# Hybrid decoder layer on one core: three first output tiles in turn instead of two, input and output moved in pairs of tiles

## The chip, the cores and the metric

One core of one Trainium2 chip runs the whole program. The metric is device time in microseconds (us) of one execution. PE is the matrix engine (TensorE), DVE the vector engine, ACT the scalar engine, POOL the GpSimd engine, SP the engine that here only issues transfers (its queue is SPq; ACT and POOL have queues of their own, ACTq and POOLq).

## The reference, cut to what matters

One layer of a decoder with three kinds of heads, on a prompt of 256 tokens and 8 samples of 8 tokens, so on T = 320 token columns, with a model width D = 2048:

```python
hn = rms_norm(x, norm_mix)
proj = hn @ w_in                      # 2048 x 6656
p_rw, p_hg, p_lru = split(proj)       # RWKV-7 | HGRN2 | RG-LRU
x = x + concat([rwkv7_mix(p_rw), hgrn2_mix(p_hg), rglru_mix(p_lru)]) @ w_out
hn = rms_norm(x, norm_ffn)
gte, val = split(hn @ ffn_w_up)       # 2 x 5632
x = x + (silu(causal_dwconv(gte)) * val) @ ffn_w_down
y = rms_norm(x, norm_final)
```

The RWKV part has 12 heads of 64 columns (a shift by one token, a low-rank decay, a normalised key, a recurrence with a delta rule), the HGRN2 part 6 heads of 128, the RG-LRU part 512 channels. All states and the results are outputs too.

## The kernel before, in words

**Tiles and chunks.** Everything is held transposed: 128 rows of a width on the partitions, the 320 tokens along the free axis. x is 16 tiles of 128x320 (k = 0 to 15). A weight matrix comes in chunks of 128x1024 values (512 KB): eight blocks of 128x128, for eight k-tiles of one output tile. `load` (L167) issues a chunk's transfer on SPq into `raw`. `split_weights` turns it into two parts: ACT casts it (`wh`, L173), DVE subtracts (`wl`, L174). The activations are split likewise into `xh` (ACT, L217) and `xl` (DVE, L218).

**A gemm.** `gemm` makes one output tile from two chunks. Per chunk it issues 16 products `wh` x `xh` and `wh` x `xl` (L198, L199) and then 8 products `wl` x `xh` (L205): 48 products of 128x128 by 128x320 for one output tile. There are 9600 of them in the program; the text calls a place in the program by how many of them stand ahead of it (its count). The result sits in a PSUM buffer of the pool `acc`, which has two, or of `aux_r`, which has four.

**Between the gemms.** All other PE work (about 1000 small fp32 products for the recurrences) is written as generators in queues named n r f h l y; `tick` (at every fourth k-tile and at the end of a chunk) lets a generator go on when its due time, kept in units of an estimated clock, has come. That fixes at which count a step's products stand in PE's stream. A scheduler then orders the instructions of each engine; what goes through `keep_in_program_order` (and `behind`, the same for a transfer on SPq) stays where it was written.

**The head.** Three idle products (L260) run on zeros. SPq issues the first chunks and the 16 tiles of x, one transfer each of 160 KB. `first_tiles` (L307, L308, L310) makes output tiles 0 and 1 (the inputs of the decay and the gate) in turn, four k-tiles at a time, so that work starts when a quarter of x is there. Their PSUM is `aux_r`. Then `rwkv_front` makes tile 3, the key of the first pair of RWKV heads, as an ordinary gemm in `acc`. Behind it stands one product of a matrix of ones with `ssq` (L401), the sum of squares of x, which gives the norm factor `rstd` (ACT L234, DVE L235). With `rstd` the function `shifted` empties the PSUM of tiles 0, 1 and 3 in that order (DVE L378, L380), then come the receptance and value tiles (2 and 4) and the tiles of the first HGRN2 head. POOL issues the loads of `shift`, `h0` and `ccv` at the start, and the loads of masks (`mskf`), `lw` and `s` go on SPq behind the norm product.

**A pair of RWKV heads.** `rwkv_pair` is run six times, alternating with the six HGRN2 heads. Its steps: low-rank products (L482), the key's norm, whose product is L502 (the text says the bones product, from the name of its matrix) with DVE L503, ACT L504 and L505 (Ln and Exp, each with a load of a function table) and DVE L510 behind it; then the operands `nb`, `a`, `BK`, `ARs` (DVE L512 to L556); the chunk products (L578), a triangular solve over 16x16 blocks whose off-diagonal blocks are moved through DRAM (`du`, `U`, L614, L615) and come back in front of PE's transposes L686; and doubling steps (L703), in which PE multiplies 64x64 blocks, ACT copies `Z` (L708) and DVE writes the result into `U` and `T` (L695, by a masked copy). The doubling steps of one pair stand beside the key's norm of the next pair.

**The end.** After the mix come the output projection, the two FFN matrices and the final norm (PE L1282, L1283; ACT L234; DVE L235, L1289, L1291); the 16 result tiles are sent by 16 transfers of 160 KB (L1292), odd ones from ACT's queue, even ones from SP's.

Of the kernel before, what the change touches and what calls it, by code (L numbers as in the profile page):

```python
# [17 lines left out]
P = 128  # L18
# [48 lines left out]
def kernel(ctx: ExitStack, tc: tile.TileContext, i: dict, o: dict):  # L67
# [30 lines left out]
    for h in range(2):  # L98
        for n in range(2):
            chunks.append((i["w_in"][n, h], 8))  # L100
    for n in [c for k, m in ORDER for c in
                       {"r": (3 + 3 * m, 2 + 3 * m, 4 + 3 * m), "h": range(20 + 4 * m, 24 + 4 * m),
                        "l": (44 + 4 * m, 46 + 4 * m, 45 + 4 * m, 47 + 4 * m)}[k]]:
        for h in range(2):
            chunks.append((i["w_in"][n, h], 8))
# [82 lines left out]

    def gemm(pieces, xh, xl, k0=0, first=True, last=True, ps=None):
        if ps is None:  # L190
            ps = acc_p.tile([P, 512], F32, tag="acc", name="acc")
        for c, kc in enumerate(pieces):
            prefetch()
            wh, wl = splits.pop(state["used"])
            state["used"] += 1
            for k in range(kc):
                st = first and c == 0 and k == 0
                PE.matmul(ps[:, :T], wh[:, k, :], xh[k0 + k], start=st, stop=False)  # L198
                PE.matmul(ps[:, :T], wh[:, k, :], xl[k0 + k], start=False, stop=False)  # L199
                state["clock"] += 2 * GEMM_COST  # L200
                if k % 4 == 3:
                    tick()
            for k in range(kc):
                en = last and c == len(pieces) - 1 and k == kc - 1
                PE.matmul(ps[:, :T], wl[:, k, :], xh[k0 + k], start=False, stop=en)  # L205
# [58 lines left out]
    xh, xl, xr = [], [], []  # L264
    ssq = et("ext", T)
# [4 lines left out]

    raws[3] = rp.tile([P, 10, P], F32, tag="big", name="raw3", bufs=BB)
    for g in range(4):
        ks = slice(4 * g % 8, 4 * g % 8 + 4)
        if g < 3:
            load(2 * (g // 2), ks)
        for k in range(4 * g, 4 * g + 4):
            t = yp.tile([P, T], F32, tag=f"y{k}", name="xr")
            SY.dma_start(out=t, in_=i["xT"][k])
            xr.append(t)
        if g == 3:  # L280
            load(2, ks)
        load(2 * (g // 2) + 1, ks)
    for g in range(4):
        ks = slice(4 * g % 8, 4 * g % 8 + 4)
        split_weights(2 * (g // 2), ks)
# [5 lines left out]
        split_weights(2 * (g // 2) + 1, ks)  # L291
        if g:
            squares(range(4 * g - 4, 4 * g) if g < 3 else ())
# [4 lines left out]
    state["raw"] = state["split"] = 4  # L298

    def first_tiles():  # L300

        pss = [aux_r(), aux_r()]
        for g in range(4):
            for n, ps in enumerate(pss):
                wh, wl = splits[2 * (g // 2) + n]
                for k in range(4 * g, 4 * g + 4):
                    PE.matmul(ps[:, :T], wh[:, k % 8, :], xh[k], start=(k == 0), stop=False)  # L307
                    PE.matmul(ps[:, :T], wh[:, k % 8, :], xl[k], start=False, stop=False)  # L308
                for k in range(4 * g, 4 * g + 4):
                    PE.matmul(ps[:, :T], wl[:, k % 8, :], xh[k], start=False, stop=(k == NK - 1))  # L310
            state["clock"] += 24 * GEMM_COST
            if g % 2:
                for n in range(2):
# [81 lines left out]
    def rwkv_front():  # L395
        ps_0, ps_1 = first_tiles()
        tc.keep_in_program_order(V.tensor_scalar(omu, prm[:, PRM["mu"]:PRM["mu"] + 20], -1.0, 1.0, op0=ALU.mult, op1=ALU.add))
        squares(range(8, NK))
        ps_k = gemm(W_CHUNKS, xh, xl)
        ps_n = aux_h()  # L400
        tc.keep_in_program_order(PE.matmul(ps_n[:, :T], ones, ssq, start=True, stop=True))  # L401
# [12 lines left out]
        free(xo)  # L414
        x, xo = shifted(1, ps_1)
        S.activation(sg, x, AF.Sigmoid)
        free(xo)
        return ps_k

# [39 lines left out]

    def rwkv_pair(p, ps_k=None):  # L460
        lw = rp.tile([P, 3, P], F32, tag="lw", name="lw", bufs=2)
# [4 lines left out]
        for name, n in (("k", 3), ("r", 2), ("v", 4)):  # L466
            ps = gemm(W_CHUNKS, xh, xl, ps=aux_r()) if p == 0 and name == "v" else ps_k
            ps_k = None
            box[name] = shifted(n + 3 * p, ps)
# [4 lines left out]
    def rwkv_operands(p, lw, box):  # L474
# [6 lines left out]
        for n, ps in enumerate((ps_w, ps_a)):  # L481
            PE.matmul(ps[:, :T], lw[half[n], n, :], lora[half[n], :], start=True, stop=True)  # L482
        sw = ft("sw")
# [337 lines left out]
    def rwkv_norm(p, lw, y, bo):  # L821
# [20 lines left out]
        PE.matmul(ps_g[:, :T], lw[:, 2, :], sg, start=True, stop=True)  # L842
        yo = yp.tile([P, T], F32, tag=f"y{p}", name="yo")
        V.tensor_tensor(yo, ps_g[:, :T], bo, op=ALU.mult)
# [32 lines left out]
    def hgrn_steps(n, box):  # L877
# [147 lines left out]
        V.tensor_tensor(rs, ps_o[:, :T], rs, op=ALU.mult)  # L1025
        yo = yp.tile([P, T], F32, tag=f"y{NPAIR + n}", name="yo")
        V.scalar_tensor_tensor(yo, rs, pc("hnw", n), g, op0=ALU.mult, op1=ALU.mult)
# [76 lines left out]
    def lru_steps(m, box):  # L1104
        tiles = (2 * m, 2 * m + 1)
        rs, ths, aes = [], [], []
        for n, (xc, _) in zip(tiles, box["x"]):
            w = rp.tile([P, 2, P], F32, tag="wg", name="wg", bufs=1)
            G.dma_start(out=w, in_=i["wg"][n])
            yield L_LRU  # L1110
# [34 lines left out]
        for j, (n, hs) in enumerate(zip(tiles, rs)):  # L1145
# [3 lines left out]
            S.activation(gt, gt, AF.Gelu_apprx_tanh)  # L1149
            yo = yp.tile([P, T], F32, tag=f"y{NPAIR + NHG + n}", name="yo")  # L1150
            hp, hs_ = extended(hs)
# [34 lines left out]

    ps_k = rwkv_front()
    spawn("y", y_steps())
    for kind, n in ORDER:
# [4 lines left out]
        if (kind, n) == ("r", 0):  # L1194
            rwkv_pair(0, ps_k)
        else:
            {"r": rwkv_pair, "h": hgrn_head, "l": lru_pair}[kind](n)
# [7 lines left out]
    def x2_tile(n, ps):  # L1205
        t = yp.tile([P, T], F32, tag=f"y{n}", name="x2")
        G.dma_start(out=t, in_=i["xT"][n])
        V.tensor_tensor(t, ps[:, :T], t, op=ALU.add)
# [77 lines left out]
    for n in range(NK):  # L1286
# [10 lines left out]
NIDLE = 3  # L1297
L_FIRST = 11.0
L_FIRST_OPS = 4.0
# [21 lines left out]
ORDER = [(k, n) for n in range(6) for k in "rh"] + [("l", 0), ("l", 1)]  # L1321
NFIRST = 4
QUEUES = "nrfhly"
BX = 1

_OUTS = {
    "yT": (NK, P, T), "p_rwkv": (NPAIR, P, 64), "s_rwkv": (NPAIR, P, SB, 64), "nshift": (P, 20, 9),
    "p_hgrn": (NHG, P, P), "s_hgrn": (NHG, P, SB, P), "nh": (P, NLRU, 9), "nccv": (P, NLRU, 9, 3),
# [140 lines left out]
```

## Time and profile before

| what | value |
| --- | --- |
| median of 3 runs | 1626.79 us (1625.04 to 1627.25) |
| the profiled execution's own time | 1627.56 us |
| its span in the trace | 1625.8 us |
| PE busy | 1601.6 us, 99% of the span |
| DVE busy | 973.9 us, 60% |
| ACT busy | 809.6 us, 50% |
| POOL busy | 144.7 us, 9% |
| DMA, mean | 147 GB/s |

The profile is of one execution; 1.76 us of its time lie around the span. A row of the timeline has the start, the duration, the engine and line, the operation, and in square brackets how long the engine had been idle and what released it. A matrix product's rows overlap, since products are pipelined: the distance from one start to the next is what it costs. An fp32 product is two passes and shows as two (x2). The granted clock of PE is 0.997 over the span.

### The profile page before, as it was taken

The page shows a single profiled execution, that of the slowest core. Times are in us where ns is not written, and L with a number is a line of the kernel's source. Part 1 is how long each engine was busy: PE and PEld are TensorE (multiplying, and loading weights), DVE is VectorE, ACT ScalarE, POOL GpSimd, SP SyncE. Part 2 cuts the span into 40 slices and gives each one's busy share as a digit, 9 for nine tenths or more (in the row PEclk, how much of TensorE's full clock was granted, in tenths as well). Part 3 has the DMA queues.
Part 4 walks back from the last instruction along what each step waited for, and adds up shares of the span by engine and source line. Part 5 has one row for each costly group of instructions (what it writes and reads, how often), then busy time and mean ns, then how long its engine had stood idle before and what let it go on. Part 6 is the DMA issues. An engine that isn't in the chain of part 4 may idle for free.

```text
span 1625.8 us, 29013 instructions
## 1 busy us (share of the span) xinstructions
PE 1601.6 (99%) x11478; PEld 1548.6 (95%) x11478; DVE 973.9 (60%) x1965; ACT 809.6 (50%) x1280; POOL 144.7 (9%) x364
## 2 busy tenths in 40 slices
PE   9999999999999999999999999999999999999996
PEld 8888989898989999999999999999999999999996
DVE  7786878777776765555555554343455555554444
ACT  7766766676766964443434343323334343344442
POOL 2101111111111300001111110000011110000000
PEclk9999999999999999999999999999999999999998
DMA  8444343444344554454445444555444444445553
GB/s 266 154 132 135 117 141 120 128 120 136 114 135 122 168 169 150 151 158 148 151 148 156 145 153 144 147 152 149 155 151 154 146 153 145 155 146 156 149 151 109
DMA packets 87791, 238.91 MB, mean 147 GB/s; under 512 B 16712, under 2 KB 31096, under 8 KB 87656
## 3 DMA queue, kind: packets, MB, share of 16 engines
q1 hardware_dynamic: 81496, 221.01, 44.4%
q0 software_dynamic: 4576, 14.16, 2.6%
q8 instruction: 90, 1.47, 0.4%
q10 hardware_dynamic: 1584, 1.89, 0.3%
q14 instruction: 45, 0.37, 0.1%
HBM read 225.66 MB, written 11.37 MB: 146 GB/s over the span
## 4 chain that ended last, share of the span: by engine, by line
PE 85%; ACT 7%; DVE 4%; DMA 2%; issue 2%; SPq 0%; POOL 0%; DVEq 0%; ACTq 0%
PE acc L198 26%; PE acc L205 26%; PE acc L199 26%; DVE wl L174 1%; PE aux_r L703 1%; PE aux_h L914 1%; ACT wh L173 1%; DMA raw<-in_w_in 1%; ACT L935 0%; ACT L893 0%; ACT L1023 0%; DVE x L1289 0%; PE aux_r L656 0%; PE aux_r L729 0%; DMA mskf<-in_msk 0%
## 5 line engine op out<-in xcount | busy, mean ns | idle before, releaser
L173 ACT CAST wh<-raw 128x1024 fp32r<-128x1024 f32 (+2 forms) x412 | 421.6, 1025 | 542.8 <-PE acc L199 338.2
L198 PE MATMUL acc<-xh,wh 128*128 128x320 f32 x2192 | 661.0, 315 | 0.0
L199 PE MATMUL acc<-xl,wh 128*128 128x320 f32 x2192 | 648.2, 309 | 0.0
L174 DVE TENSOR_TENSOR wl<-raw,wh 128x1024 fp32r<-128x1024 f32 (+2 forms) x412 | 489.9, 1190 | 224.5 <-ACT wh L173 113.1
L198 PEld LDWEIGHTS acc<-xh,wh 128*128 128x128 f32 x2192 | 411.7, 188 | 13.6 <-issue 10.7
L199 PEld LDWEIGHTS acc<-xl,wh 128*128 128x128 f32 x2192 | 411.7, 188 | 1.3
L205 PE MATMUL acc<-xh,wl 128*128 128x320 f32 x2192 | 372.6, 312 | 0.0
L205 PEld LDWEIGHTS acc<-xh,wl 128*128 128x128 f32 x2192 | 332.3, 188 | 2.8
L198 PE MATMUL acc<-hh,wh 128*128 128x320 f32 x704 | 207.9, 308 | 0.0
L199 PE MATMUL acc<-hl,wh 128*128 128x320 f32 x704 | 207.9, 308 | 0.0
L199 PEld LDWEIGHTS acc<-hl,wh 128*128 128x128 f32 x704 | 132.1, 188 | 0.0
L198 PEld LDWEIGHTS acc<-hh,wh 128*128 128x128 f32 x704 | 131.7, 187 | 0.0
L205 PE MATMUL acc<-hh,wl 128*128 128x320 f32 x704 | 118.8, 308 | 0.0
L1251 POOL COPY ncch<-fe 128x18 f32<-128x18 f32 x44 | 49.7, 1131 | 652.7 <-DVE fe L1250 652.7
L205 PEld LDWEIGHTS acc<-hh,wl 128*128 128x128 f32 x704 | 107.1, 187 | 0.0
L1261 DVE TENSOR_TENSOR fv<-acc,rstd 128x320 f32<-128x320 f32 x44 | 21.6, 492 | 98.5 <-PE acc L205 98.5
L1249 DVE TENSOR_TENSOR fe<-acc,rstd 128x256 f32<-128x256 f32 x44 | 18.7, 425 | 99.6 <-PE acc L205 99.6
L214 ACT CAST hh<-fv 128x320 fp32r<-128x320 f32 x44 | 20.3, 460 | 96.9 <-DVE fv L1263 96.9
L198 PE MATMUL acc<-yhl,wh 128*128 128x320 f32 x224 | 66.2, 310 | 0.0
L199 PE MATMUL acc<-yhl,wh 128*128 128x320 f32 x224 | 66.0, 307 | 0.0
L1256 DVE SCALAR_TENSOR_TENSOR fc<-fe,prm,fc 128x336 f32<-128x336 f32 x88 | 49.8, 566 | 1.6
L1254 ACT ACTIVATE fc<-fe,prm 128x336 f32<-128x336 f32 x44 | 29.4, 669 | 35.7 <-DVE fe L1250 35.7
(416 smaller groups left out, 1616.6 us busy)
## 6 DMA issues: line engine op xcount, KB each, us to landing
raw<-in_w_up SPq DMA_DIRECT2D x176, 512.0 KB, 3.5
raw<-in_w_in SPq DMA_DIRECT2D x100, 512.0 KB, 3.5
raw<-in_w_dn SPq DMA_DIRECT2D x64, 512.0 KB, 3.4
raw<-in_w_out SPq DMA_DIRECT2D x32, 512.0 KB, 3.6
raw<-in_w_dn SPq DMA_DIRECT2D x32, 384.0 KB, 3.0
out_s_hgrn<-hs POOLq DMA_DIRECT2D x12, 256.0 KB, 4.6
xr<-in_xT SPq DMA_DIRECT2D x16, 160.0 KB, 3.8
hs<-in_hs POOLq DMA_DIRECT2D x10, 256.0 KB, 4.2
```

What stands on the lines that cost most here:

```text
L173: S.copy(wh[:, ks, :], raws[n][:, ks, :])
L174: V.tensor_tensor(wl[:, ks, :], raws[n][:, ks, :], wh[:, ks, :].bitcast(F32), op=ALU.subtract)
L198: PE.matmul(ps[:, :T], wh[:, k, :], xh[k0 + k], start=st, stop=False)
L199: PE.matmul(ps[:, :T], wh[:, k, :], xl[k0 + k], start=False, stop=False)
L205: PE.matmul(ps[:, :T], wl[:, k, :], xh[k0 + k], start=False, stop=en)
L214: S.copy(xh, src)
L703: PE.matmul(ps[q, b * 64:(b + 1) * 64], lhs[q, b, q], r[q], start=True, stop=True)
L1249: V.tensor_tensor(e[:, 2:258], ps[:, 0:TP], rstd[:, 0:TP], op=ALU.mult)
L1251: G.tensor_copy(ncch[:, j], e[:, 248:EX].rearrange("p (b s) -> p b s", s=10)[:, :, 8:10])
L1254: S.activation(c[:, 0:N], e[:, 0:N], AF.Identity, scale=pc("fw", 3 * j), bias=pc("fb", j))
L1256: V.scalar_tensor_tensor(c[:, 0:N], e[:, m:m + N], pc("fw", 3 * j + m), c[:, 0:N], op0=ALU.mult, op1=ALU.add)
L1261: V.tensor_tensor(val, ps[:, :T], rstd, op=ALU.mult)
```

## The change

- `first_tiles` makes three output tiles in turn: 0, 1 and 3. The third (the first pair's key) has an `acc` buffer and is no gemm of its own any more. Chunks are loaded in that order, and the two further raw chunks of the head have buffers of their own.
- x is loaded in pairs of tiles (320 KB each). The first pair comes in two: x0 together with the norm weights (one transfer of 168 KB), then x1.
- Two more idle products stand behind the first two products (those of k = 0).
- The norm product stands inside the receptance tile's gemm, ahead of its last 8 products (`within`).
- `shift`, `h0` and `ccv` move from POOL's queue at the start to SPq behind, and one load of `wg` too; `prm` and `cst` are issued on ACT's queue after all splits of the head.
- The first pair's low-rank products are kept where they are written.
- The result tiles leave in 8 transfers of 320 KB, one for each pair, in turn from SP's and ACT's queue. The 16 tiles of x, y and x2 live in one tile `yall`.
- `L_FIRST`, a due time of the first pair's steps, is 6 instead of 11.

```diff
-    def gemm(pieces, xh, xl, k0=0, first=True, last=True, ps=None):
+    def gemm(pieces, xh, xl, k0=0, first=True, last=True, ps=None, within=None):
...
+            if within and c == len(pieces) - 1:
+                within()
...
-    nmix = cp.tile([P, NK], F32, tag="nmix", name="nmix")
-    S.dma_start(out=nmix, in_=i["prm"][:, PRM["nmix"]:PRM["nmix"] + NK])
+    x0 = et("diff", NK + T)
+    nmix = x0[:, 0:NK]
+    yall = yp.tile([P, NK, T], F32, tag="yall", name="yall")
...
+        load(first, ks)
+        if g == 0:
+            SY.dma_start(out=x0, in_=i["x0"])
+            SY.dma_start(out=yall[:, 1, :], in_=i["xP"][0, :, 1, :])
+        for m in range(2 * g, 2 * g + 2):
+            if m:
+                SY.dma_start(out=yall[:, 2 * m:2 * m + 2, :], in_=i["xP"][m])
+        for n in range(1, NF):
+            load(first + n, ks)
...
-        if g == 1:
-            tc.keep_in_program_order(S.dma_start(out=prm, in_=i["prm"]))
-        if g == 2:
-            tc.keep_in_program_order(S.dma_start(out=cst, in_=i["cst"]))
+    tc.keep_in_program_order(S.dma_start(out=cst, in_=i["cst"]))
+    tc.keep_in_program_order(S.dma_start(out=prm, in_=i["prm"]))
...
-        pss = [aux_r(), aux_r()]
+        pss = [aux_r(), aux_r(), acc_p.tile([P, 512], F32, tag="acc", name="acc")]
...
+                    if n == 0 and k == 0:
+                        for _ in range(NIDLE2):
+                            tc.keep_in_program_order(PE.matmul(ps_i[:, :T], idle[:, 0:P], idle, start=True, stop=True))
...
-    G.dma_start(out=shift, in_=i["shift"])
...
-    G.dma_start(out=h0, in_=i["h0"])
...
-    G.dma_start(out=ccv, in_=i["ccv"])
...
-        ps_0, ps_1 = first_tiles()
+        ps_0, ps_1, ps_k = first_tiles()
...
-        ps_k = gemm(W_CHUNKS, xh, xl)
+        behind(out=shift, in_=i["shift"])
         ps_n = aux_h()
-        tc.keep_in_program_order(PE.matmul(ps_n[:, :T], ones, ssq, start=True, stop=True))
+        ps_r = gemm(W_CHUNKS, xh, xl, within=lambda: tc.keep_in_program_order(
+            PE.matmul(ps_n[:, :T], ones, ssq, start=True, stop=True)))
...
+        behind(out=h0, in_=i["h0"])
+        behind(out=ccv, in_=i["ccv"])
...
+            pin = tc.keep_in_program_order if p == 0 else lambda ins: ins
+            pin(PE.matmul(ps[:, :T], lw[half[n], n, :], lora[half[n], :], start=True, stop=True))
...
-        (S if n % 2 else SY).dma_start(out=o["yT"][n], in_=y)
+        if n % 2:
+            (S if n % 4 == 3 else SY).dma_start(out=o["yP"][n // 2], in_=yall[:, n - 1:n + 1, :])
...
+NIDLE2 = 2
-L_FIRST = 11.0
+L_FIRST = 6.0
+FIRST_TILES = (0, 1, 3)
```

What it does to the order shows at two places. The first is PE's stream around the norm product, which reads `ext` (the sum of squares) and writes `aux_h`. Before, with the last products of tile 3 ahead of it and the first ones of the receptance tile behind it:

```order
L205 MATMUL acc<-xh_240,wl 128x320
L205 MATMUL acc<-xh_244,wl 128x320
L205 MATMUL acc<-xh_248,wl 128x320
L401 MATMUL aux_h<-ext,cst 128x320
L198 MATMUL acc<-xh_146,wh 128x320
L199 MATMUL acc<-xl_147,wh 128x320
```

After, where the line of the same product is L410:

```order
L198 MATMUL acc<-xh_239,wh 128x320
L199 MATMUL acc<-xl_240,wh 128x320
L410 MATMUL aux_h<-ext,cst 128x320
L207 MATMUL acc<-xh_189,wl 128x320
L207 MATMUL acc<-xh_193,wl 128x320
L207 MATMUL acc<-xh_197,wl 128x320
```

It moved from count 144 to count 184. The steps of the first pair stand later with it: the low-rank products at count 248 (before 240), the bones product at 264 (256), the first chunk products at 344 (336). From there on the RWKV steps stand 8 products later than before, while the steps of the HGRN2 heads keep their counts.

The second place is DVE's stream where the key's norm of the second pair (`kn`, `nb`, `a`, `ARs`, `BK`) meets the doubling steps of the first (`U`, `T`); the same pattern stands at four more pairs. Before:

```order
L503 TENSOR_SCALAR kn<-aux_r 128x320
L974 TENSOR_TENSOR kd<-hk,x 128x320
L510 SCALAR_TENSOR_TENSOR kn<-xs,prm,kn 128x320
L695 COPY_PREDICATED U<-msk,aux_r 128x16x16
L512 SCALAR_TENSOR_TENSOR nb<-kn,a 128x320
L695 COPY_PREDICATED T<-msk,aux_r 128x16x16
L514 TENSOR_SCALAR a<-a,prm 128x320
L532 TENSOR_TENSOR BK<-nb,cum 128x2x64
```

After (L521 is the former L503, L528 the former L510, L713 the former L695):

```order
L521 TENSOR_SCALAR kn<-aux_r 128x320
L992 TENSOR_TENSOR kd<-hk,x 128x320
L528 SCALAR_TENSOR_TENSOR kn<-xs,prm,kn 128x320
L530 SCALAR_TENSOR_TENSOR nb<-kn,a 128x320
L574 TENSOR_TENSOR ARs<-kn,ep 64x2x32
L532 TENSOR_SCALAR a<-a,prm 128x320
L550 TENSOR_TENSOR BK<-nb,cum 128x2x64
L533 SCALAR_TENSOR_TENSOR a<-a,xs 128x320
L551 TENSOR_TENSOR BK<-nb,cum 128x2x64
L550 TENSOR_TENSOR BK<-a,cum 128x2x64
L551 TENSOR_TENSOR BK<-a,cum 128x2x64
L713 COPY_PREDICATED U<-msk,aux_r 128x16x16
```

The masked copy into `T` is the row behind the last one. Both copies stood among the first four steps of the series and now stand behind all of it. In PE's stream the bones product comes 24 gemm products ahead of the doubling step that reads `T` before, and 32 ahead of it after, with one more small burst (the products `cst`,`hv` of the HGRN2 head) between.

More of the change, by code (lines that the diff above doesn't have):

```diff
@@ L98 @@
     for h in range(2):
-        for n in range(2):
+        for n in FIRST_TILES:
             chunks.append((i["w_in"][n, h], 8))
@@ L269, in squares @@
             add_square(ssq, xr[k], k, lambda: rp.tile([P, T], F32, tag="c", name="sq", bufs=BC))
-    raws[3] = rp.tile([P, 10, P], F32, tag="big", name="raw3", bufs=BB)
+    NF = len(FIRST_TILES)
+    for n in (NF, NF + 1):
+        raws[n] = rp.tile([P, 10, P], F32, tag="big", name=f"raw{n}", bufs=BB)
     for g in range(4):
         ks = slice(4 * g % 8, 4 * g % 8 + 4)
[L274 to L282, printed above, removed]
+        first = NF * (g // 2)
+        load(first, ks)
[7 more added lines that the diff above has]
+            load(first + n, ks)
+    xr = [yall[:, k, :] if k else x0[:, NK:NK + T] for k in range(NK)]
     for g in range(4):
         ks = slice(4 * g % 8, 4 * g % 8 + 4)
-        split_weights(2 * (g // 2), ks)
+        first = NF * (g // 2)
+        split_weights(first, ks)
         for k in range(4 * g, 4 * g + 4):
@@ L290 @@
             xl.append(b)
-        split_weights(2 * (g // 2) + 1, ks)
-        if g:
-            squares(range(4 * g - 4, 4 * g) if g < 3 else ())
-        if g == 1:
-            tc.keep_in_program_order(S.dma_start(out=prm, in_=i["prm"]))
-        if g == 2:
-            tc.keep_in_program_order(S.dma_start(out=cst, in_=i["cst"]))
-    state["raw"] = state["split"] = 4
+        for n in range(1, NF):
+            split_weights(first + n, ks)
+        if g in (1, 2):
+            squares(range(4 * g - 4, 4 * g))
+    tc.keep_in_program_order(S.dma_start(out=cst, in_=i["cst"]))
+    tc.keep_in_program_order(S.dma_start(out=prm, in_=i["prm"]))
+    state["raw"] = state["split"] = 2 * NF
     def first_tiles():
-        pss = [aux_r(), aux_r()]
+        pss = [aux_r(), aux_r(), acc_p.tile([P, 512], F32, tag="acc", name="acc")]
         for g in range(4):
             for n, ps in enumerate(pss):
-                wh, wl = splits[2 * (g // 2) + n]
+                wh, wl = splits[NF * (g // 2) + n]
                 for k in range(4 * g, 4 * g + 4):
@@ L308, in first_tiles @@
                     PE.matmul(ps[:, :T], wh[:, k % 8, :], xl[k], start=False, stop=False)
+                    if n == 0 and k == 0:
+                        for _ in range(NIDLE2):
+                            tc.keep_in_program_order(PE.matmul(ps_i[:, :T], idle[:, 0:P], idle, start=True, stop=True))
                 for k in range(4 * g, 4 * g + 4):
                     PE.matmul(ps[:, :T], wl[:, k % 8, :], xh[k], start=False, stop=(k == NK - 1))
-            state["clock"] += 24 * GEMM_COST
+            state["clock"] += 12 * NF * GEMM_COST
             if g % 2:
-                for n in range(2):
+                for n in range(NF):
                     splits.pop(state["used"])
@@ L417, in rwkv_front @@
         free(xo)
-        return ps_k
+        return ps_k, ps_r
     STEP = 16 * P + 16
@@ L466, in rwkv_pair @@
         for name, n in (("k", 3), ("r", 2), ("v", 4)):
-            ps = gemm(W_CHUNKS, xh, xl, ps=aux_r()) if p == 0 and name == "v" else ps_k
-            ps_k = None
+            if p:
+                ps = None
+            elif name == "k":
+                ps = ps_k
+            elif name == "r":
+                ps = ps_r
+            else:
+                ps = gemm(W_CHUNKS, xh, xl, ps=aux_r())
             box[name] = shifted(n + 3 * p, ps)
@@ L1149, in lru_steps @@
             S.activation(gt, gt, AF.Gelu_apprx_tanh)
-            yo = yp.tile([P, T], F32, tag=f"y{NPAIR + NHG + n}", name="yo")
+            yo = yall[:, NPAIR + NHG + n, :]
             hp, hs_ = extended(hs)
@@ L1205, in x2_tile @@
     def x2_tile(n, ps):
-        t = yp.tile([P, T], F32, tag=f"y{n}", name="x2")
-        G.dma_start(out=t, in_=i["xT"][n])
+        t = yall[:, n, :]
+        G.dma_start(out=t, in_=i["xP"][n // 2, :, n % 2, :])
         V.tensor_tensor(t, ps[:, :T], t, op=ALU.add)
@@ L1430 @@
     arrays = {
-        "xT": x.T.reshape(NK, P, T),
+        "xP": x.T.reshape(NK // 2, 2, P, T).transpose(0, 2, 1, 3),
+        "x0": np.concatenate([prm["nmix"], x.T[0:P]], axis=1),
         "w_in": chunked(w_in), "w_out": chunked(w_out), "w_up": w_up, "w_dn": w_dn,
```

21 lines of the change are left out of this document (10 added, 11 removed).

## The prediction

> **What bounds the kernel now.** I read the profile's page first: busy time by engine and the chain that ended last.
>
> ```profile
> span 1625.8 us, 29013 instructions
> ...
> PE 1601.6 (99%) x11478; PEld 1548.6 (95%) x11478; DVE 973.9 (60%) x1965; ACT 809.6 (50%) x1280; POOL 144.7 (9%) x364
> ...
> PE 85%; ACT 7%; DVE 4%; DMA 2%; issue 2%; SPq 0%; POOL 0%; DVEq 0%; ACTq 0%
> ```
>
> PE is busy for all but 24.2 us, so only two things can move the time: what PE does, and the few places where it stands still. The second view is therefore the list of PE's own waits (line waited at, what released it, total, times, longest):
>
> ```profile
> PE aux_r L781 <- DVE sbd L794: 2.3, 5, 0.6
> ...
> PE aux_r L307 <- ACT xh L217: 1.4, 2, 1.1
> PE aux_r L502 <- ACT kn L499: 1.2, 1, 1.2
> PE aux_r L686 <- DMA U<-du: 1.0, 1, 1.0
> ```
>
> Nothing there is larger than 2.3 us. The head of the program, which the change rewrites, holds 1.4 us of it at L307, and 0.85 at the norm product (L401 in the next rows). So the change can win two or three us there; a new wait that comes back with every pair of heads can cost as much. The third view is PE's timeline of the head:
>
> ```profile
> 1.38 3.57 PE L260 MATMUL aux_h<-idle 128*128 128x320 f32 x6 [1.38 <-DVE idle L257]
> 4.70 0.63 PE L307 MATMUL aux_r<-xh,wh 128*128 128x320 f32 x1
> 5.43 0.63 PE L308 MATMUL aux_r<-xl,wh 128*128 128x320 f32 x1
> 7.18 0.64 PE L307 MATMUL aux_r<-xh,wh 128*128 128x320 f32 x1 [1.12 <-ACT xh L217]
> ...
> 8.20 0.47 PE L307 MATMUL aux_r<-xh,wh 128*128 128x320 f32 x1
> 8.47 0.47 PE L308 MATMUL aux_r<-xl,wh 128*128 128x320 f32 x1
> ...
> 10.57 0.31 PE L308 MATMUL aux_r<-xl,wh 128*128 128x320 f32 x1
> 10.71 0.32 PE L307 MATMUL aux_r<-xh,wh 128*128 128x320 f32 x1
> ...
> 30.04 1.33 PE L205 MATMUL acc<-xh,wl 128*128 128x320 f32 x8
> 32.22 0.81 PE L401 MATMUL aux_h<-ext,cst 128*128 128x320 f32 x2 [0.85 <-DVE ext L253]
> 32.62 0.55 PE L198 MATMUL acc<-xh,wh 128*128 128x320 f32 x1
> 33.01 0.31 PE L199 MATMUL acc<-xl,wh 128*128 128x320 f32 x1
> ...
> 39.90 0.31 PE L198 MATMUL aux_r<-xh,wh 128*128 128x320 f32 x1
> ```
>
> Two rates show. At 8.20 to 8.47 products follow each other by 0.27 us, from about 10.5 on by 0.147 (10.57 to 10.71 and on): a product is twice as slow in the first ten us. 4.70 to 7.18 is two products and a wait for the second tile of x.
>
> **The change part by part.** All sums are made against the profiled execution (span 1625.8 us, 1627.56 with what lies around it), which is 0.77 us above the median of 1626.79.
>
> *The head, to the end of the third tile.* Before, the last product of tile 3 is issued at 30.04 + 7 x 0.147 = 31.07, so it ends near 31.2. After, the two products of k = 0 end near 6.06 as now (5.43 + 0.63). The two added idle products are four fp32 passes; the three at the start take 3.57 us for six (first row above), 0.595 each, so the fill lasts 2.4 us, to 8.4. The second tile of x was split by 7.18, so nothing waits there. Of 142 further products eight go at 0.27 (to 10.5), 134 at 0.147 (19.7): 30.2. That is 1.0 us earlier. If full rate comes 3.4 us after 4.70 rather than after 7.18 (7.18 to 10.57 is 3.4; the fill closes the gap that made it 7.18), it is 8.4 + 142 x 0.147 = 29.3, 1.9 earlier. I take 1.5. [...]
>
> Does data keep up with three tiles per quarter of x? It must, or the fill and the third tile only wait. A quarter now feeds 36 products, 5.3 us, instead of 24. The stretches of the window view (PE busy, PEld, DVE, ACT, POOL with counts, clock, share of the DMA engines, GB/s) show the demand:
>
> ```profile
> 5.00:10.00 5.00, 3.79 (x11) 2.81 (x11) 3.21 (x8) 3.45 (x9) 1.58 (x8) 1.00 0.97 339
> 10.00:15.00 5.00, 5.00 (x35) 5.00 (x34) 5.00 (x12) 5.00 (x12) 0.00 (x0) 1.00 1.06 374
> ```
>
> Three tiles of weights are 3.1 MB and x is 2.6 MB; at 339 to 374 GB/s 5.8 MB take 16 to 17 us, so the last is there before 20, and the last group of products starts near 25. Pairs of x and the loads taken off POOL's queue change nothing that is late: their cost is zero here, and if this cover were gone, one late pair costs about the 1.1 us that L307 waits now.
>
> *The norm product.* Before, PE loses 31.2 to 32.87 to it: 1.65 us, of which 0.54 is the product (two passes of 0.27) and the rest is a wait for the squares. After, it stands 40 products (5.9 us) later, so the 0.85 us of lateness is covered: 1.1 us won. Together 2.6 by the first product of the value tile (39.90, now near 37.3).
>
> *What comes late in its place.* Everything that needs `rstd` starts at the norm product, which now ends at 37.3 - 8 x 0.147 = 36.1 instead of 33.0. The key tile lies in one of two `acc` buffers, and is emptied by:
>
> ```profile
> 42.27 0.22 DVE L380 TENSOR_TENSOR ext<-acc,rstd 128x64 f32<-128x64 f32 x1
> ```
>
> and PE's own later rows are
>
> ```profile
> 51.57 0.81 PE L502 MATMUL aux_r<-kn,cst 128*128 128x320 f32 x2 [1.19 <-ACT kn L499]
> ...
> 64.03 1.16 PE L578 MATMUL aux_r<-AR,BK 64*128 64x128 f32 x16
> ...
> 97.41 0.66 PE L686 MATMUL aux_r<-cst,U 128*128 128x128 f32 x4 [0.99 <-DMA U<-du]
> ```
>
> The key's buffer is free 9.5 us behind the norm product (42.49 - 33.0), so at 45.6 after. PE wants that buffer for the first tile of the HGRN2 head one gemm (48 x 0.147 = 7.04) behind 37.3, at 44.3. A new wait of 1.3 us; queued behind it is all of PE's stream. Bounds 0.5 to 3: the masks' loads, `h0` and `ccv` now share SPq ahead of `lw`, which can push this chain. In return the bones product comes 8 products later and behind this wait, 2.5 us in all, so its 1.19 goes: -1.2 (bounds -1.2 and 0). Net by the first chunk products: -1.5 - 1.1 + 1.3 - 1.2 = -2.5.
>
> The next meeting point is `U` coming back through DRAM: 64.03 to 97.41, 33.4 us, ends in a wait of 0.99. DVE work and two transfers make this chain, PE's products only fill it. If nothing in it changes, the wait stays and the 2.5 survive; but the RWKV steps now stand 8 products (1.2 us) later against HGRN2 steps on the same DVE and ACT, whose places did not move, and each of DVE's two long stretches can lose a place. Bounds 0 and 3, I take +1.5.
>
> *The doubling steps.* Here the order costs most. The first of the five pairs that do this, on PE, DVE and ACT:
>
> ```profile
> 102.08 0.70 PE L502 MATMUL aux_r<-kn,cst 128*128 128x320 f32 x2
> ...
> 102.76 0.31 PE L199 MATMUL acc<-xl,wh 128*128 128x320 f32 x1
> ...
> 105.20 0.39 PE L198 MATMUL acc<-xh,wh 128*128 128x320 f32 x1
> 105.44 0.31 PE L199 MATMUL acc<-xl,wh 128*128 128x320 f32 x1
> ...
> 108.15 0.68 PE L703 MATMUL aux_r<-T,mt 64*64 64x64 f32 x16 [0.35 <-DVE T L695]
> 108.76 0.44 PE L991 MATMUL aux_h<-cst,hv 128*128 128x128 f32 x2
> ...
> 109.06 0.39 PE L198 MATMUL acc<-xh,wh 128*128 128x320 f32 x1
> ```
>
> ```profile
> 106.38 0.55 DVE L510 SCALAR_TENSOR_TENSOR kn<-xs,prm,kn 128x320 f32<-128x320 f32 x1 [2.02 <-ACT kn L505]
> ...
> 107.58 0.42 DVE L695 COPY_PREDICATED T<-msk,aux_r 128x256 f32<-128x256 uint8 x1
> ...
> 109.41 0.42 DVE L378 TENSOR_TENSOR ext<-acc,rstd 128x256 f32<-128x256 f32 x1
> ```
>
> ```profile
> 101.27 0.35 ACT L708 COPY Z<-aux_r 128x256 f32<-128x256 f32 x1
> ...
> 103.99 0.47 ACT L504 ACTIVATE kn<-kn 128x320 f32<-128x320 f32 x1 [0.18 <-DVE kn L503]
> ```
>
> PE reaches the step that reads `T` 5.72 us behind the bones product (108.15 - 0.35 - 102.08). After, 8 products more (1.2) and one burst (108.76 to 109.06, 0.30) lie between: 7.2 to 7.3. DVE reaches L510 4.30 behind the bones product. From there to the end of the series, both masked copies among it, is 3.03 (106.38 to 109.41). After, the same steps run in another order with `T` last, and with one piece of `ARs` more (64 columns; at most a third of a copy's 0.42, so 0.15), and the last step counts to its end rather than to the next one's start, about 0.1: 3.28. Then 0.15 from the end of `T` (108.00) to PE's start. Sum 4.30 + 3.28 + 0.15 = 7.7. And ACT: the doubling step that feeds `Z` (L708) now stands right ahead of the bones product, so the copy of 101.27 comes about 0.9 later; the Ln of 103.99 and its table load stand behind it on ACT, and the time to spare there is 0.18 us, with some 0.3 more in the small steps between: about 0.4 late. 8.1 against 7.3 is a wait of 0.8 us, 0.3 and 1.1 being the bounds. Five pairs: 4.0, less the 0.35 that is there now: +3.65 (1.2 to 5.2). [...]
>
> *More switches.* The auxiliary products now stand at 33 more places among the gemms. A switch costs nothing behind the bones product (102.08 to 102.76 is two passes of 0.27 and one product of 0.147), and about 0.09 behind the small blocks (105.20 to 105.44 instead of 0.147). 33 x 0 to 0.1: 0 to 3.3, I take 1.65.
>
> *The end.* Eight stores instead of sixteen:
>
> ```profile
> 1616.11 6.12 DVE L1289 TENSOR_TENSOR x<-x,rstd 128x320 f32<-128x320 f32 x15
> ```
>
> DVE makes a tile every 0.41 us (6.12 over 15), so the first store starts one tile later, while the last one can only start with the last tile either way and is twice as long: 0, bounds -0.4 and +0.4.
>
> **Sum:** -2.5 + 1.5 + 3.65 + 1.65 + 0 = +4.3 us: 1631.9 for a profiled execution like this one, 1631.1 against the median.
>
> **The rivals.** About 0.2%, 3.25 us, is what a measurement of this kernel can tell from no change; so faster is below 1623.5, slower above 1630.0.
>
> *The head's gain comes through (faster).* It needs the doubling steps' wait to vanish: DVE's 7.7 to 8.1 us against PE's 7.3 is a margin of 0.4 to 0.8, so PE's path only has to be longer, or the series shorter, by that. Then -2.5 - 0.35 = -2.9: 1623.9, at the edge of what counts as faster; with the early full rate (2.6 instead of 1.5), 1622.8. For it: before, the same wait shows only once, 0.35. Against it: five copies moved behind the rest of a series of 3 us. Chance 0.13. The early full rate by itself has a chance of 0.25 and moves any case by -1.1.
>
> *Gain and waits cancel (same).* The `U` wait stays at 0.99 and switches are free: -2.5 + 3.65 = +1.2, 1628.0. For it: nothing in that chain is lengthened on paper, and no switch behind a full-size product costs anything. Chance 0.30.
>
> *The front chain is late too (slower still).* SPq now carries `shift`, `h0`, `ccv` and one `wg` between masks and `lw`; the release of the key tile slips to the bound of 3, the bones wait stays, the `U` wait takes its 3: -2.6 + 3 + 0 + 3 + 3.65 + 1.65 = +8.7, 1635.5. Chance 0.12.
>
> **How the numbers follow.** My forecast, 1631.1, has 0.45, its own range 1629 to 1633.5. With it the slower cases have 0.57, the same 0.30, the faster 0.13. The range to hold 8 in 10 reaches from just below the cancelling case's low side to just above the late chain: 1624.5 to 1637.
>
> **What would show it.** In the profile after: the third tile's last product near 30; the norm product (L410) without a wait; a wait of about a us for a PSUM buffer at the first HGRN2 tile near 45; the row for L704 on `U` above 0.99; five waits of 0.8 at L721 on `T`, which decide between the first two rivals and the forecast. If PE has no wait on `T`, or the head is over 3 us earlier at the pairs, I am wrong.

## The result and the profile after

The changed kernel takes 1639.26 us (median of 3 runs, 1636.65 to 1639.51) against 1626.79 us: 1.0069 times the time of the kernel before, 95% interval 1.0055 to 1.0083. That is 12.5 us slower, where +4.3 was forecast and 1637.0 was the upper end of the range. The profiled execution is the one of 1639.26 us. Its page:

```profile
span 1637.5 us, 28962 instructions
...
PE 1602.3 (98%) x11482; PEld 1552.1 (95%) x11482; DVE 976.1 (60%) x1967; ACT 807.7 (49%) x1282; POOL 143.4 (9%) x360
```

PE's busy time is what it was, 1602.3 us against 1601.6; PE stands still for 35.2 us instead of 24.2. Its waits say where (us in total, times, longest):

```profile
PE aux_r L721 <- DVE T L713: 4.7, 5, 0.9
PE aux_r L799 <- DVE sbd L812: 4.4, 5, 0.9
PE aux_r L843 <- DVE y L828: 2.5, 1, 2.5
PE aux_r L665 <- ACT uv L652: 2.4, 5, 0.5
PE acc L198 <- DVE ext L388: 2.3, 1, 2.3
PE aux_r L704 <- DMA U<-du: 2.2, 1, 2.2
PE acc L207 <- DVE wl L174: 1.7, 1, 1.7
```

Three of these rows come five times, once for each pair that has a next one: `T` (forecast), `sbd` (2.3 in total before, as L781) and `uv` (not there before). Four come once: the last pair's `y`, the key tile's buffer (`ext`), `U`, and a weight split (`wl`). The wait on the squares at the norm product and the one on the second tile of x are gone.

PE's head, where the change was meant to act:

```profile
5.18 0.64 PE L316 MATMUL aux_r<-xl,wh 128*128 128x320 f32 x1
5.61 1.74 PE L319 MATMUL aux_h<-idle 128*128 128x320 f32 x4
6.95 0.56 PE L315 MATMUL aux_r<-xh,wh 128*128 128x320 f32 x1
7.34 0.30 PE L316 MATMUL aux_r<-xl,wh 128*128 128x320 f32 x1
7.48 0.39 PE L315 MATMUL aux_r<-xh,wh 128*128 128x320 f32 x1
...
34.49 0.70 PE L410 MATMUL aux_h<-ext,cst 128*128 128x320 f32 x2
```

The fill is 1.74 us long instead of the 2.4 reckoned, and the products behind it already follow each other by 0.147 us (7.34 to 7.48): full rate came before 7, not at 10.5. In the trace's record of the granted clock, full speed begins at 10.51 us before and at 6.62 after.

The same place in the program can be compared in both traces by its count of gemm products. The table is worked out from the two timelines: the start of the product with that count, after minus before, in us. A place is only fair where both kernels have issued the same small products as well; from count 192 on the rows are such places (the added idle products apart). At count 576, for example, the changed kernel still has 24 small products ahead of it that the kernel before has behind it, so its +0.52 there hides 1.9 us that come by count 600.

| count | before | after | difference | what happened since the row above |
| --- | --- | --- | --- | --- |
| 36 | 13.95 | 12.78 | -1.17 | early full rate |
| 144 | 32.62 | 28.62 | -4.01 | no gaps behind x, norm product not yet due |
| 192 | 39.90 | 36.20 | -3.70 | norm product without a wait |
| 480 | 95.59 | 94.68 | -0.92 | key buffer 2.27, weight split 1.72, bones wait of 1.19 gone |
| 600 | 127.64 | 130.02 | +2.38 | `U` 2.19 instead of 0.99, first wait on `T`, a slow stretch |
| 2352 | 543.08 | 550.51 | +7.43 | five periods of two heads |
| 2400 | 552.59 | 563.23 | +10.64 | last y 2.47 instead of 0.62, a slow stretch |
| 9000 | 1523.28 | 1534.46 | +11.19 | output projection, 0.05 a tile |

The last 0.5 us of the 11.7 lie behind the start of the last step on DVE. A slow stretch is one in which the products follow each other at half rate, 0.27 us apart instead of 0.147; the experiments come back to it.

### The profile page after: what moved, and what is told of

It reads as the page before. It is cut to its first block, busy times and chain, and to the rows that moved or that the text cites. A ratio compares the mean times of both kernels' runs of the same rounds, so it can differ in the third digit from the quotient of the medians.

```text
span 1637.5 us, 28962 instructions
## 1 busy us (share of the span) xinstructions
PE 1602.3 (98%) x11482; PEld 1552.1 (95%) x11482; DVE 976.1 (60%) x1967; ACT 807.7 (49%) x1282; POOL 143.4 (9%) x360
## 4 chain that ended last, share of the span: by engine, by line
PE 85%; ACT 7%; DVE 3%; DMA 2%; issue 1%; POOL 0%; SPq 0%; DVEq 0%; ACTq 0%; POOLq 0%
PE acc L198 26%; PE acc L207 26%; PE acc L199 26%; ACT wh L173 1%; PE aux_h L932 1%; PE aux_r L721 1%; DMA raw<-in_w_in 0%; ACT L911 0%; ACT L853 0%; ACT L1042 0%; ACT L522 0%; DMA mskf<-in_msk 0%; DVE yall L1307 0%; PE aux_h L1066 0%; ACT L1041 0%
## 5 line engine op out<-in xcount | busy, mean ns | idle before, releaser
L207 PEld LDWEIGHTS acc<-xh,wl 128*128 128x128 f32 x2176 | 329.0, 188 | 5.2 <-DVE wl L174 2.2
```

## The experiments

Medians in us, with the ratio to the kernel before, timed on the same chip. "Places" are the counts at which the first pair's chunk products stand, and with them the later RWKV steps.

| run | places | time | ratio, 95% interval |
| --- | --- | --- | --- |
| changed, L_FIRST 5 | 336, as before | 1627.23 | 0.9999 (0.9990 to 1.0009) |
| before, L_FIRST 12 | 344, as changed | 1633.93 | 1.0040 (1.0025 to 1.0055) |
| changed, L_FIRST 3 | 320 | 1625.48 | 0.9988 (0.9978 to 0.9997) |
| changed, no fill | 344 | 1638.69 | 1.0071 (1.0056 to 1.0086) |
| L_FIRST 3, lw early | 320 | 1627.37 | 1.0001 (0.9992 to 1.0010) |
| the same, single stores | 320 | 1626.55 | 0.9998 (0.9989 to 1.0007) |
| before, fill | 336 | 1625.96 | 0.9994 (0.9985 to 1.0003) |
| before, L_FIRST 9 | 320 | 1626.94 | 1.0000 (0.9991 to 1.0009) |
| L_FIRST 3, lw and norm early | 320 | 1627.25 | 1.0003 (0.9994 to 1.0012) |
| L_FIRST 5, lw and norm early | 336 | 1627.62 | 1.0007 (0.9998 to 1.0016) |
| changed, no fill, work in the wait | 344 | 1640.1 | a single run |
| changed, again | 344 | 1637.08 | 1.0069 (1.0056 to 1.0082) |

### The places of the RWKV steps

My theory after the result: it is not the head, the stores or the loads that cost, but that the RWKV steps stand 8 products later against the HGRN2 steps. Not quite all of them do: the low-rank and bones products of the later pairs keep their counts (440, 504, 776, 840 and so on) in both kernels, and what stands 8 later is each pair's chunk products and everything behind them. The due time L_FIRST moves these as a block, and at 5 (changed) and 12 (before) they stand at each other's counts. So the two kernels can be given each other's places.

```diff
-L_FIRST = 6.0
+L_FIRST = 5.0
```

> The changed kernel with the due time L_FIRST at 5 instead of 6. The first pair's steps, and with them all RWKV steps, stand 8 products earlier: exactly at the counts of the kernel before (336 for the first chunk products), and DVE's copies of U and T stand behind the fourth-last steps of the series again. Theory A, that the place of the RWKV steps against the HGRN2 steps makes the loss: the waits on T (5 x 0.93), the longer ones on sbd and uv and the 2.47 at the last y product go, the head's gain stays, and the time is 1623 to 1627. Theory B, that the later norm chain and the loads now on SP's queue make the loss, wherever the steps stand: the waits move to the first pair and the time stays above 1634. Theory C, that T's copies alone matter: 5 x 0.86 = 4.3 less, 1635.

Measured: 1627.23, no difference from before, 12 us less than the changed kernel. Its waits:

```profile
PE aux_r L799 <- DVE sbd L812: 2.3, 5, 0.6
PE aux_r L500 <- DMA lw<-in_lw: 2.1, 1, 2.1
...
PE aux_r L843 <- DVE y L828: 0.6, 1, 0.6
PE aux_r L721 <- DVE T L713: 0.6, 1, 0.6
```

`uv` is gone, `sbd` is back to its 2.3 of before, `T` waits once. From count 528 to 2496 this kernel keeps its distance to the kernel before within 0.1 us. Theories B and C are out: the first by the time, the second because `sbd`, `uv` and the last y left together with `T`. The head's gain was not seen in the time, though. The lw row shows a first place where it went, and behind that wait the products stand 0.27 us apart from 47.59 to 50.52 us, a second one.

```diff
-L_FIRST = 11.0
+L_FIRST = 12.0
```

> The kernel before with L_FIRST at 12 instead of 11, nothing else: its RWKV steps stand at the counts of the changed kernel (344 for the first chunk products), with its own head, loads and stores. Theory A: the loss of the changed kernel from its count 480 on comes back without the change, some 1.5 us for each of five pairs and 3 us at the last pair's y, so 1636 to 1640. Theory B: the steps have room, no more than 2 us slower, 1627 to 1629.

Measured: 1633.93, 7 us slower, less than the 1636 to 1640 expected, but far over the 1629 of theory B. The three rows come back in a kernel that has nothing else of the change:

```profile
PE aux_r L703 <- DVE T L695: 4.6, 5, 0.9
PE aux_r L781 <- DVE sbd L794: 4.4, 5, 0.9
PE aux_r L647 <- ACT uv L634: 2.6, 5, 0.5
PE aux_r L502 <- ACT kn L499: 2.3, 1, 2.3
...
PE aux_r L825 <- DVE y L810: 1.2, 1, 1.2
```

From count 600 to 2352 it loses 4.93 us (+2.05 to +6.98); the changed kernel loses 5.05 there (+2.38 to +7.43). So the five periods belong to the places alone. Of the 2.05 ahead of them, 1.07 is the bones wait (2.26 instead of 1.19), and 0.74 lies in the head, where its products are those of the kernel before, so I take that for scatter. What it does not have is the rest of the changed kernel's loss at the end of the mix: 0.58 us between 2352 and 2400 against 3.21.

> The changed kernel with L_FIRST at 3: RWKV steps 24 products earlier than in the changed kernel at the chunk products (320), DVE's copies of U and T ahead of the whole series of the next pair. Theory A: no wait on T, less on sbd; but the first pair's products may be due before the key tile is emptied, 1 to 3 us at the first bones product: 1623 to 1628. Theory B: the earlier the steps the longer the first waits, 1638 or more.

Here the edit is L_FIRST = 3 in the changed kernel. Measured: 1625.48, 0.9988 of before: the only version whose interval lies below the kernel before, by some 2 us (0.12%). No wait on `T` or `sbd` is left; in their place PE waits for `bkt` of the sample states, 1.8 in five times, and 2.6 for lw, with products 0.27 us apart right behind (47.53 to 49.93).

> The kernel before with L_FIRST at 9 instead of 11: the RWKV steps stand 16 products earlier, at the places that the changed kernel with L_FIRST at 3 has from the first chunk products on (320). If the places make that kernel's gain over L_FIRST at 5 (1.75 us): the pairs win 1 to 2 us here too, and the first pair, which is not ready so early, loses 1 to 3 at the bones product or the low-rank products: 1625 to 1628. If the gain there is the head's: 1628 to 1630.

The kernel before with L_FIRST at 9 took 1626.94, no difference. The pairs win 0.8 us from count 624 to 2304 (+1.44 to +0.62), and the first pairs lose it, with 2.7 us of waiting for lw and 1.4 for a weight split. So the earlier places are worth about 1 us in the pairs, and it seems that a head that is earlier is needed to take them; no run separates the two.

### Where the head's gain goes

> The kernel before with the two idle products behind its first two, nothing else. Clock theory: full rate comes near 7 instead of 10.5 us, the first 36 products are done 1.2 us earlier (as 12.8 stands against 13.95). But the norm product then waits longer for the squares, which the fill does not hurry: the gain is gone at L401, and the time is 1626.5 to 1627.5. If the squares are no bound: 1625.5.

Edit: two products on the idle tile behind the first two products of the kernel before. Measured: 1625.96, 0.9994 (0.9985 to 1.0003): no difference that the interval can tell, and 1.5 us less in the profile's counts. There the norm product waited 0.7 us, not longer, so my reason for no gain was wrong. The 1.5 us can't be put on the fill alone, since the head differs from one execution to the next. With the same products up to count 144 as the kernel before, the run with L_FIRST 12 was 0.74 us later there and the one with L_FIRST 9 1.21 earlier, so the 0.74 that this run is earlier there lies within the scatter. What the fill does show is early full rate: in the timelines of seven runs with the fill the first products 0.147 us apart come at 7.2 to 8.8 us, in the five without it only at 10.6 to 13.9, and the seven are 0.6 to 1.2 us earlier at count 36 than the kernel before, while the four other runs without it are 0.1 to 1.3 later.

> The changed kernel with L_FIRST at 3, and the first pair's lw loaded ahead of the masks instead of behind masks, zeros, h0 and ccv on SP's queue. In the run with L_FIRST at 3 PE stood still for 2.56 us at the low-rank products for that load. If the load alone is what eats the head's gain: 1.5 to 2.5 us less than that run's 1625.5, so 1623 to 1624. Rival: the norm chain is late behind it anyway (the key tile is emptied 9.5 us behind the norm product), and the wait moves to the next step of the first pair: 1625 to 1626.

```diff
+        lw0.append(rp.tile([P, 3, P], F32, tag="lw", name="lw", bufs=2))
+        behind(out=lw0[0], in_=i["lw"][0])
         for n in range(0, NMSK, T):
```

Measured: 1627.37, no better than without the edit (the intervals of the ratios, 0.9992 to 1.0010 and 0.9978 to 0.9997, just overlap). The rival was right; the wait moved to the key tile's buffer:

```profile
PE acc L198 <- DVE ext L388: 3.8, 1, 3.8
...
PE aux_r L507 <- DMA lw<-in_lw: 0.6, 1, 0.6
```

> The changed kernel with L_FIRST at 3, lw early, and the norm product 16 products earlier, ahead of the last chunk of the receptance tile (count 168) instead of ahead of its last 8 products (184). The squares are summed by 30.0 us in the run with lw early, the product would stand near 32.4, so nothing new waits. If the chain norm product to key tile's buffer is what eats the head's gain: the wait of 3.77 us falls by 2.3, and the time by as much against that run's 1627.4: 1625. If the next thing behind it (lw, the bones product) is late too: 1626.5 or more.

```diff
-            if within and c == len(pieces) - 1:
-                within()
             (the same two lines, ahead of the loop over the chunk's first 16 products)
```

Measured: 1627.25. The key buffer's wait is gone and two others stand there:

```profile
PE aux_r L507 <- DMA lw<-in_lw: 2.0, 1, 2.0
...
PE aux_r L527 <- ACT kn L524: 1.8, 1, 1.8
```

> The same with L_FIRST at 5, so with the pairs' steps at the places of the kernel before. The run with L_FIRST at 5 alone took 1627.2, with 2.1 us of waiting for lw. With lw early and the norm product early the two waits of the first pair that the other runs showed are both shortened: 1625 to 1626 if the head's gain is kept in part, 1627 if a third wait takes it.

Measured: 1627.62, with 2.6 us at the bones product. At count 240 these last two are 2.95 and 3.54 us ahead of the kernel before, at 480 they are 0.57 and 1.07 behind it; of the second, 0.34 us ahead is left at 528, behind the wait on `U`. So four different rows (lw, the key's buffer, the bones product's `kn`, the second pair's lw) took the head's gain in turn, each as the one before it was cleared. Waits are not all of it: in four other timelines with L_FIRST 3 or 5 (each of the two alone, lw early, lw and norm early) a slow stretch, products 0.27 us apart, follows one of these waits (2.0 to 3.8 us); in the changed kernel such stretches cost 1.69 and 1.36 us. My reading is that the first pair's chain, not PE, sets when the first pair ends, and that it begins at the norm product; moving that product by 16 places moved the wait but not the time, which fits and does not prove it.

> The kernel with lw early, and the result stored tile by tile (16 stores of 160 KB) as in the kernel before, instead of in pairs. If the pairs cost the 0.5 us by which the changed kernel's span is longer from the last DVE step on: 0.3 to 0.6 less than the kernel with lw early. If that difference is the DMA's own scatter: the same.

Edit: each result tile stored alone into its half of the pair. Measured: 1626.55 against 1627.37, intervals that overlap. The time from the start of DVE's last step to the end of the span is 4.4 us here, 4.1 with pairs (3.6 before): the pairs are not what made the end longer. It is 4.1 to 4.4 in all ten profiles with the change and 3.6 in all four without. The cause stays open.

### The slow stretches

> The changed kernel without its two added idle products in the head (NIDLE2 = 0), the order otherwise the same. If the fill is what brought full rate at 7 us instead of 10.5, the head is slower by about 1.3 to 1.6 us (some 10 products at twice the pitch, less the fill's own time that waited for x anyway); half of it may be covered by the wait on the key's buffer, since the norm chain starts later by as much: 1639.5 to 1641. If the fill does nothing: 1638 to 1639.3.

Measured: 1638.69, no difference from the changed kernel's 1639.26 and 1637.08, whose runs spread too far to show a head that is 1 or 2 us later. But the counts of the profiled executions tell more: 2.46 us later than the changed kernel at count 36, another 1.52 between 240 and 264, and 2.66 won back between 2352 and 2400. The second of these in its timeline:

```profile
48.05 0.60 PE L198 MATMUL acc<-xh,wh 128*128 128x320 f32 x1 [2.19 <-DVE ext L388]
48.45 0.47 PE L199 MATMUL acc<-xl,wh 128*128 128x320 f32 x1
48.71 0.47 PE L198 MATMUL acc<-xh,wh 128*128 128x320 f32 x1
```

and at the same place in the changed kernel, with a wait as long:

```profile
45.67 0.38 PE L198 MATMUL acc<-xh,wh 128*128 128x320 f32 x1 [2.27 <-DVE ext L388]
45.89 0.30 PE L199 MATMUL acc<-xl,wh 128*128 128x320 f32 x1
46.03 0.31 PE L198 MATMUL acc<-xh,wh 128*128 128x320 f32 x1
```

Behind the one the products follow by 0.27 us, behind the other by 0.147. The stretch view (PE busy, PEld, DVE, ACT, POOL, granted clock, DMA share, GB/s) shows it in the granted clock:

```profile
45.00:50.00 5.00, 2.81 (x13) 2.58 (x13) 3.19 (x8) 4.46 (x7) 2.37 (x9) 0.80 0.97 277
50.00:55.00 5.00, 5.00 (x27) 3.81 (x27) 3.24 (x10) 3.23 (x6) 0.87 (x6) 0.86 0.49 201
```

In the changed kernel's profile the clock of both stretches is 1.00.

> The changed kernel without the fill in the head, and with four products of constants (2.2 us of PE work, result unused) ahead of the first HGRN2 tile, where PE stood still for 2.2 us and then ran at twice the pitch for 3.4 us. If standing still is what halves the clock: no products of 0.27 us pitch behind it, and the 1.5 us that were lost between counts 240 and 264 are not lost. If the slow stretch has another cause (transfers, power): it stays.

```diff
+        if n == 0:
+            ps_f = aux_h()
+            for _ in range(4):
+                tc.keep_in_program_order(PE.matmul(ps_f[:, :T], ones, m01[:, :T], start=True, stop=True))
         box = {"q": projected("hq")}
```

Its timeline at that place:

```profile
44.77 2.31 PE L888 MATMUL aux_h<-m,cst 128*128 128x320 f32 x8
47.13 0.38 PE L198 MATMUL acc<-xh,wh 128*128 128x320 f32 x1
47.35 0.31 PE L199 MATMUL acc<-xl,wh 128*128 128x320 f32 x1
47.50 0.31 PE L198 MATMUL acc<-xh,wh 128*128 128x320 f32 x1
```

With work in the wait the slow stretch is gone, and so are the 1.5 us (against the changed kernel 1.46 later at 240, 1.45 at 264). The time of this single run says nothing, since another slow stretch came (behind `U`). And by itself it does not show the cause, since the changed kernel had no slow stretch at this place either, with a wait of 2.27.

> The changed kernel once more, for the last y product alone: its first profile had a wait of 2.47 us there behind a store that took 4.1 us, and a stretch at half rate behind that, 2.7 us together, while two other runs had 1.2 us. If that store's landing differs from one execution to the next: the runs spread over 1636.5 to 1639.5, and this profile shows either 2.5 or 1.2. If it is fixed in this kernel: 1639 in all runs, and 2.5 again.

Measured: 1635.23 to 1640.94, median 1637.08, and 2.47 again: the runs spread, but not by this wait. The store of the state (`s`) makes it longer: the chain that ends at the last y runs from the store's landing over ACT, which stands still for it,

```profile
541.08 0.46 ACT L216 CAST yhl<-yall 128x320 fp32r<-128x320 f32 x1 [1.50 <-DMA out_s_rwkv<-s]
```

and the store, issued at 537.02, took 3.98 us to land. ACT stands still for that landing for 1.5, 1.4 and 1.9 us in the three profiles with 2.47 (the changed kernel's two and the one with work in the wait), and has no such wait in the two with 1.2 (no fill, and before with L_FIRST 12). What differs between the two profiles is what follows the wait. In the first:

```profile
556.66 1.41 PE L843 MATMUL aux_r<-y,cst 128*128 128x320 f32 x2 [2.47 <-DVE y L828]
557.40 0.94 PE L198 MATMUL acc<-xh,wh 128*128 128x320 f32 x1
558.13 0.47 PE L199 MATMUL acc<-xl,wh 128*128 128x320 f32 x1
558.40 0.47 PE L198 MATMUL acc<-xh,wh 128*128 128x320 f32 x1
```

and in the second:

```profile
555.27 0.78 PE L843 MATMUL aux_r<-y,cst 128*128 128x320 f32 x2 [2.47 <-DVE y L828]
555.64 0.55 PE L198 MATMUL acc<-xh,wh 128*128 128x320 f32 x1
556.03 0.31 PE L199 MATMUL acc<-xl,wh 128*128 128x320 f32 x1
556.18 0.31 PE L198 MATMUL acc<-xh,wh 128*128 128x320 f32 x1
```

1.36 us between them. The second profile has its slow stretch behind the key buffer's wait instead (1.52 us between counts 240 and 264), and none behind `U`, where the first had one (1.69 us between 480 and 528). These two come from the difference of the two timelines by count, as in the table above.

Where the slow stretches lie can be read more closely from the first profile's record of the granted clock. Full speed begins at 6.62 us, half speed at 98.78 and at 556.16, which is 27 and 161 times 3.413 us later, and each time it lasts 3.41 us; the next half speed begins at 1627.95, behind PE's last products. Cut from 6.62 on into pieces of 3.413 us, PE stood still for 2.19 us in the piece that ends at 98.78 and for 1.97 in the one that ends at 556.16, and for 1.51 or less in every other piece up to its last products. The wait on the key's buffer (2.27 us, 43.40 to 45.67), which no half speed followed, falls into two pieces, 0.76 and 1.51. In the kernel before, PE stood still for 1.10 us at most in one such piece behind its head, and the record has full speed from 10.51 to 1614.78 us. So in the first profile it is not the length of a wait alone that goes with half speed, but also where the wait falls. This is read from one profile with slow stretches; no run tested it by moving a wait, and why the second profile's 2.47 has none behind it was not shown.

## Why the prediction was wrong, step by step

The direction, slower, was right; the size was not. One step had the wrong mechanism, and three things were not in the sum: a wait for a weight split, the last y, and the slow stretches. By the prediction's own steps, for the profiled executions:

- *The head.* 2.6 us won by the value tile was forecast; 3.70 was measured (count 192). The early full rate that I left to a rival is what happened. No run shows the term of 2.6 by which the rival and its chance reckoned it, an estimate of mine; in its place the traces show full speed from 10.51 us on before, 3.3 us behind the end of the gap at 7.18, and with the gap filled 3.9 us sooner, at 6.62, and the third tile's last product issued 2.6 us earlier (28.47 instead of 31.07).
- *The key's buffer, the bones wait, `U`.* Forecast +1.3, -1.2, +1.5; the rows say +2.27, -1.19 and, for `U`, +1.20 (2.19 instead of 0.99), and a wait of 1.72 for a weight split was not foreseen. With the head and the first of the waits on `T` (0.8 - 0.35), -0.55 was forecast up to here; measured is +2.38 at count 600, of which 1.69 is a slow stretch: +0.69 without it. The sum was 1.2 us too low: the weight split's wait and the longer wait on the key's buffer outweigh the better head. Why DVE's weight split came late there I did not find out.
- *`T`.* Forecast a wait of 0.8, five times; measured 0.93, five times (4.7). The working held to 0.15 us, in its parts too (L528 is 4.71 us behind the bones product, 4.7 forecast; from there to the end of `T` 3.38, 3.28 forecast):

```profile
103.84 0.81 PE L520 MATMUL aux_r<-kn,cst 128*128 128x320 f32 x2
...
112.08 0.68 PE L721 MATMUL aux_r<-T,mt 64*64 64x64 f32 x16 [0.93 <-DVE T L713]
```

8.24 us from the bones product to the step that reads `T`, where 8.1 was forecast, and 7.31 without the wait (7.3).

- *More switches.* Here the mechanism failed. I took the steps' later places as a cost per switch, 33 x 0.05 = 1.65, and looked for waits at one place only. The places also lengthened the wait on `sbd` by 2.1 and made one on `uv` of 2.4. For counts 600 to 2352 the forecast comes to four waits on `T` and the switches, 3.2 + 1.65 = 4.85, and 5.05 was measured: that is luck. The four waits on `T` are 3.7; with 2.1 and 2.4 these waits come to 8.2, some smaller waits of before (1.4) are gone, and PE's own work took 1.8 us less there although it has 26 more switches. One of the rows that would have warned me was in the profile of before: `sbd` waited 0.42 to 0.64 at each of five pairs already, so that chain had no room. `uv` had no row before; the move of 8 products (1.2 us) used up the room that it had.
- *The last y.* Not in the sum at all: the wait at the last pair's y went from 0.62 to 2.47, 1.85 us: 0.6 by the places (1.2 in the kernel before with L_FIRST 12), the rest by the store, which took 3.98 us to land. The row stood in the waits of before:

```profile
PE aux_r L825 <- DVE y L810: 0.6, 1, 0.6
```

- *Slow stretches.* Not in the sum: 1.69 + 1.36 = 3.05 us in the profiled execution, the largest single miss. The sum took full rate for granted behind every new wait.
- *The end.* Forecast 0 within 0.4; measured 0.5, and 0.55 more in the output projection, where a tile takes 0.05 us longer between counts 2730 and 3220 in every kernel that has the change's tile for y. I did not find why.

Sum: 0.69 + 1.69 + 5.05 + 1.85 + 1.36 + 0.55 + 0.5 = 11.7 us, the difference of the spans. Against the 4.3 forecast, 7.4 are missing: 3.05 of slow stretches, 1.85 at the last y, 1.24 ahead of count 600, 1.05 in the output projection and at the end, and 0.2 in the five periods. Without the slow stretches the time would be, by an estimate from these rows, 1636.2, inside the range, but still with the wrong mechanism for the periods.

The rival on the slower side, a late front chain, gave 1635.5 by another mechanism. Only part of it happened in the changed kernel (the key's buffer 2.27 of its 3, `U` 1.2 of its 3, the bones wait gone), but late first-pair waits are what ate much of the head's gain once the places were set right. The rival on the faster side (-2.5 - 0.35) set the terms for `U` and the switches to nothing without a reason, so it was reckoned some 3 us too fast for what it assumed.

## What to carry to other kernels

A change that moves a whole family of steps against another on shared engines must be checked at every wait that the family already has, not only at the one whose order visibly changed: a wait that is there each period means no room, and each period pays. It must also be checked at steps that wait nowhere yet, as `uv` here. Undo such a shift first (one number here) before judging the rest of a change. A gain at the head was here worth only what the next data chain let through; find the step at which that chain ends and see whether it began earlier. And when two kernels are compared by count, take places at which both have issued the same work.

## What the runs showed of the hardware

- In the changed kernel's first profile PE's granted clock was at half from 98.78 to 102.19 us, behind a wait of 2.19, and from 556.16 to 559.58, from within a wait of 2.47 on, with products 0.27 us apart instead of 0.147; the two stretches cost 1.69 and 1.36 us. In the timelines of this case, behind the head, products 0.27 us apart followed ten waits of 1.95 to 3.77 us, and none of 1.78 or less; five waits of 2.08 to 2.61 had none behind them either. In the kernel before, whose longest wait past its start is 1.19, the clock stays full from 10.51 to 1614.78 us. Work of no use in such a wait (four products, 2.31 us) kept the pitch at 0.147 us behind it, in the one run that tried it; without it the pitch was 0.27.
- The changed kernel took from 1635.2 to 1640.9 us in eight runs. Its two profiles have their slow stretches in different places, 3.05 us in all in the first, and no single profile of it is worth more than those 3 us.
